# Decoder block on one core: order of loads at the turn to the last projection, a third pair of gate buffers, and the place of the last right operand's split

## The chip, the cores and the metric

The kernel runs on one core of a Trainium2 chip. The core has TensorE (PE) for matrix products, VectorE (DVE), ScalarE (ACT) and GpSimd (POOL) for elementwise work, SyncE (SP), which here only issues DMAs, and 16 DMA engines that all queues share. Each engine works through its own queue in order; semaphores tie the queues together. TensorE writes to eight banks of PSUM.

The metric is the device time of the program in microseconds (us), the median over runs. Before the change it is 2260.27 us, the median of 3 runs (2259.36 to 2262.28).

## The reference, cut to what matters

One layer, batch 1, 2048 positions, width 1024, all float32. What matters here is the end of it:

```python
proj = h @ w_in[l]
x_rnn, z_rnn, q, k, v, z_attn, g_r, g_a = jnp.split(proj, IN_SPLITS, axis=-1)
...
y_rnn = (hr * jax.nn.silu(z_rnn.astype(jnp.float32))).astype(dt) @ w_out_rnn[l]
...
o = dilated_attention_mixture(qh, kh, vh).reshape(B, S, D_ATTN)
y_attn = (o * jax.nn.silu(z_attn.astype(jnp.float32))).astype(dt) @ w_out_attn[l]
merged = jax.nn.sigmoid(g_r + bg_r) * y_rnn + jax.nn.sigmoid(g_a + bg_a) * y_attn
x = x + gate[:, None, :] * (merged @ w_o[l])
...
return rms_norm(x, g_final)
```

So there are three products of 2048 x 1024 by 1024 x 1024 at the end: the recurrent branch's output projection, the attention branch's, and the output product with `w_o`. Between them stand the two sigmoid gates and a sum.

## The kernel before

**Numbers.** A float32 product is made of three products on rounded halves: each operand is split into a high half (ScalarE, `hi_act`, line 158) and a low half, the rest (GpSimd `lo_pool`, line 164, or VectorE `lo_dve`, line 167). `mm3` then issues high·high, high·low and low·high (all through line 150). Tiles are 128 partitions by 512 float32, 256 KB.

**Stages.** First come norm, input projection and recurrence; their results go to DRAM scratch: the gated recurrent rows `yaT`, the sigmoid gates `grT` and `gaT`, and so on. Then attention, head by head; its gated outputs go to `oT`. Under attention and after it run the two output projections as fillers, and last the product with `w_o`, which uses seven products in place of eight for each 2 x 2 block (the names X, Z, W, V, Y are its PSUM banks).

**The fill, `steps` (lines 1781 to 1928).** It is a generator that issues one step of three matmuls at a time. Eight jobs, each 512 columns: jobs 0 to 3 project `yaT` and write `mrT` (recurrent branch times its gate), jobs 4 to 7 project `oT` and write `meT`, the merged sum. A job has eight tiles `m` of 128 output rows, and a tile has eight steps `k`, one for each block of 128 input rows. Jobs 0 to 5 go one after the other (tiles 0 to 47). The last two jobs, 6 and 7, share their weights and are interleaved (tiles 48 to 63): (6,0) (6,1) (7,0) (7,1) (6,2) (7,2) and so on to (6,6) (7,6) (7,7) (6,7). The change calls tile 47 `TURN`. PSUM banks alternate between two of a pool `pj`; among the last sixteen tiles every third and fourth uses the Z and W banks of the output products.

In each tile the generator also issues, at fixed steps and thus in a fixed place of each engine's queue:

- `load_w`: half a tile's weight, 512 KB, already split, from the scratch `wD`, two tiles ahead in halves (`u + 3`). It goes into one of four buffers S0 to S3 and must wait until the products that read the old content are done. From number 100 on (`RAW_W`) weights come unsplit (`rw`, three buffers) and are split on the spot (`split_w`).
- `load_y`, `split_y`: the 128 x 512 row blocks of the next job; some go through four raw buffers R0 to R3, each free when the split of its last content is done. Job 7's halves lie in the space of four right operands (`F`).
- `load_g(t)` at step 3: the gates of tile t, `grT` alone in jobs 0 to 3, later `gaT` and `mrT`, into four buffers `fg` (two pairs).
- `evict(t - 1)` (VectorE): PSUM times gate (line 1857), plus the recurrent part (line 1859), in place in the gate buffer.
- `store(t - 1)`: that buffer to `mrT` or `meT` (line 1864). Its buffer is free for a new load when the store has landed.

All these DMAs stand in the one queue of SP, in the order of issue. When one waits for its buffer, all behind it wait.

**The output products, `output_products` (lines 1943 to 2205).** While the last 128 steps (tiles 48 to 63) run, `steps_at` adds work at given steps: the seven right operands are loaded in 28 parts (`load_o`, four buffers `or`), in the order `B11, T2, T3, T1, B21, T4, B22`; parts of B11, B21 and B22 are multiplied by the residual gate (`gate_o`, VectorE, line 1976); then `hi_o` (ScalarE) and `lo_o` (even parts GpSimd, odd parts VectorE). The last operand, B22, is parts 24 to 27; its product is the last of each block, and for the first block it runs behind the first product of the second block. The left operands are read from `meT` (`raw`, line 2025), summed (lines 2036, 2037, 2046, 2048) and split, by the list `jobs`, which `run_jobs(n)` works off behind product n; negative numbers stand for steps of the fill. `load_x` brings the residual rows `xo` (line 2042). `add_x` (GpSimd, line 2169) and `finish` (VectorE, line 2108 or 2140) add the products to them; the sums u2 and u3 are lines 2182 and 2187.

The lines on which the change works, as they were:

```python
if k == 3:
    load_g(t)
...
if k in (1, 2):
    load_y(j + 1, k + 4)
if k == 2:
    load_y(j + 1, KT - 1)
...
late_parts = [(0, load_o, 27)]
for i in range(24, 28):
    late_parts += [(d + (i - 24) // 2, fn, i) for d, fn in ((1, gate_o), (2, hi_o), (3, lo_o))]
```

Of the kernel before, what the change touches and what calls it, by code (L numbers as in the profile page):

```python
# [20 lines left out]
P = 128  # L21
# [68 lines left out]
def decoder_block(ctx, tc, x, c, positions, g_norm, w_mod, b_mod, w_in, b_gate, conv_w, conv_b,  # L90
# [1690 lines left out]
    def steps(jobs):  # L1781
# [1 line left out]
        tiles = [(j, m) for j in range(LAST_HEAD) for m in range(KT)]  # L1783
        tiles += [(LAST_HEAD + i, m) for i in range(2) for m in range(2)]
        tiles += [(LAST_HEAD + (i ^ (m == KT - 1)), m) for m in range(2, KT) for i in range(2)]
        Y, G = {}, {}

        raw_at, split_at = {}, {}
        for x in range(RAW_W, 2 * KT * (LAST_HEAD + 1)):
# [55 lines left out]
        def load_g(t):  # L1845
            j, m = tiles[t]
            w, ys, n = jobs[j]
            at_ = slice(m * P, (m + 1) * P), slice(n * CH, (n + 1) * CH)
            G[t] = []
            for src in (grT,) if ys is yaT else (gaT, mrT):  # L1850
                g = T(fl, [P, CH], F32, "fg", bufs=4)
                nc.sync.dma_start(g[:], src[at_])
                G[t].append(g)

# [15 lines left out]
        for t, (j, m) in enumerate(tiles):  # L1870
            ps = T(pj, [P, CH], F32, "pj") if j < LAST_HEAD or t % 4 < 2 else FP["bank"](t % 4 - 2)
            for k in range(KT):
                u = 2 * t + k // KH
                if k % KH == 1:
                    if u + 3 < RAW_W - 1:
                        load_w(u + 3)
                    elif u == 2 * KT * LAST_HEAD:
                        load_w(RAW_W - 1)
                    if u in raw_at:
                        load_w(raw_at[u])  # L1880
                    if u in split_at:
                        split_w(split_at[u])
                if k == (1 if j < LAST_HEAD else 3) and t:
                    evict(t - 1, last)
                if k == 3:
                    load_g(t)
                if k == (7 if j < LAST_HEAD else 6) and t:
                    store(t - 1)
# [8 lines left out]
                if j < LAST_HEAD:  # L1897
                    if step in range(KT * KT - 24, KT * KT - 14, 2):
                        load_y(j + 1, (step - KT * KT + 24) // 2)
                    if step == KT * KT - KT - 1:  # L1900
                        split_y(j + 1, 0)
                    if m == KT - 1:
                        if k < 4:
                            split_y(j + 1, k + 1)
                        if j + 1 < LAST_HEAD:
                            if 4 <= k < KT - 1:
                                load_y(j + 1, k + 1)
                        else:
                            if k in (1, 2):
                                load_y(j + 1, k + 4)  # L1910
                            if k == 2:
                                load_y(j + 1, KT - 1)
                            if k == KT - 1:
                                split_y(j + 1, KT - 1)
                    if j and m == 0 and k in (0, 2, 3):
                        split_y(j, 5 + (k + 1) // 2)
                else:
                    i = (t - KT * LAST_HEAD) * KT + k
                    if i < 2:
                        split_y(j, 5 + i)  # L1920
# [22 lines left out]
    def output_products(fill):  # L1943
# [19 lines left out]

        def load_o(i):
            part, k = O_PART[B_ORDER[i // KH]], i % KH
            raw_o[i] = T(fp, [P, CH], F32, "or", bufs=4)
            if isinstance(part, int):
                nc.sync.dma_start(raw_o[i][:], oD[k, :, part, :])
            else:
                rows, cols = (slice(n * d, (n + 1) * d) for n, d in ((part[0] * KH + k, P), (part[1], CH)))  # L1970
                nc.sync.dma_start(raw_o[i][:], w_o[0, rows, cols])

        def gate_o(i):
            part = O_PART[B_ORDER[i // KH]]
            if not isinstance(part, int):
                tt(raw_o[i][:], raw_o[i][:], gate_b[:, part[1] * CH : (part[1] + 1) * CH], ALU.mult)

        def hi_o(i):
            name, k = B_ORDER[i // KH], i % KH
            if k == 0:  # L1980
                F[name] = f_tile(), f_tile()
            hi_act(F[name][0][:, k, :], raw_o[i][:])

        def lo_o(i):
            name, k = B_ORDER[i // KH], i % KH
            (lo_dve if i % 2 else lo_pool)(F[name][1][:, k, :], raw_o.pop(i)[:], F[name][0][:, k, :])
# [290 lines left out]
```

## Time and profile before

| | |
|---|---|
| median of 3 runs | 2260.27 us (2259.36 to 2262.28) |
| time of the profiled execution | 2258.11 us |
| its span, first to last instruction | 2256.0 us |
| granted clock of TensorE, mean | 0.992 |
| DMA, mean rate over the span | 231 GB/s |
| TensorE busy, 2000 to 2050 us of the span | 49.13 of 50 us |
| DMA engines busy, same stretch | 0.91, 280 GB/s |

Some names for reading the lines: `S<-wD` is a split weight, `rw<-in_w_out_attn_dram` a raw one, `R<-oT` a row block of attention outputs (in 1980 to 2010) and `R<-meT` a left operand, `fg<-gaT` and `fg<-mrT` the gate pair, `meT<-fg` the store of a finished tile, `or<-...` a part of a right operand, `F` a right operand's halves, `xo` the residual rows. "SPq" marks a DMA's issue on SP's queue, with start and length of the issue; the number in brackets at an instruction is the idle time of its engine just before it, with what ended it. Times count from the first instruction.

### The profile page before, as it was taken

What the parts mean: (1) busy time and instruction counts of PE and PEld (TensorE: products, weight loads), DVE (VectorE), ACT (ScalarE), POOL (GpSimd) and SP (SyncE); (2) the same over time, 40 slices, a digit from 0 to 9 for tenths busy, and PEclk for the clock granted to TensorE, in tenths of its full rate; (3) what the DMA queues carried; (4) which work ended last, traced back from release to release, by engine and by line L of the source; (5) the groups of instructions that cost most, each with busy time, mean ns of one, the idle gap of its engine ahead of it and who ended that gap; (6) DMA issues with size and microseconds to landing.
All of it is one profiled execution on the core that took longest, in us unless ns stands there. A gap on an engine that the chain in (4) does not pass through costs nothing.

```text
span 2256.0 us, 34354 instructions
## 1 busy us (share of the span) xinstructions
PE 2201.3 (98%) x11359; PEld 1845.6 (82%) x11359; DVE 1456.7 (65%) x2451; ACT 1294.0 (57%) x2560; POOL 1215.1 (54%) x902
## 2 busy tenths in 40 slices
PE   8999999999999999999999999999999999999898
PEld 5998888888877988888888887888989898977786
DVE  5578788778557664555645455467677878645776
ACT  3547767678533436666766611477677887632333
POOL 2277677676556344445445312356565656433786
PEclk9999999999999999999999999999999999999999
DMA  8354665565797647877787899989988888788553
GB/s 283 90 171 165 204 212 179 189 228 189 233 268 230 219 138 224 260 233 237 241 256 237 261 309 296 298 266 289 272 280 264 241 261 257 234 275 260 174 168 131
DMA packets 455433, 520.19 MB, mean 231 GB/s; under 512 B 90360, under 2 KB 333268, under 8 KB 454232
## 3 DMA queue, kind: packets, MB, share of 16 engines
q1 hardware_dynamic: 427492, 434.95, 63.6%
q10 hardware_dynamic: 27572, 83.00, 9.7%
q8 instruction: 90, 1.47, 0.3%
q14 instruction: 87, 0.71, 0.1%
q0 software_dynamic: 192, 0.05, 0.0%
HBM read 340.67 MB, written 177.21 MB: 230 GB/s over the span
## 4 chain that ended last, share of the span: by engine, by line
PE 48%; DMA 10%; DVE 3%; issue 3%; ACT 2%; POOL 2%; SPq 1%; ACTq 0%; POOLq 0%; DVEq 0%
PE X L150 9%; PE pj L150 9%; PE V L150 7%; PE W L150 4%; PE Z L150 4%; PE Y L150 4%; PE sc L150 4%; PE o L150 4%; DMA fg<-mrT 1%; DMA meT<-fg 1%; PE pg L150 1%; PE pT L1628 1%; DMA wo<-in_w_o_dram 1%; PE pT L1641 1%; DMA R<-in_w_in_dram 1%
## 5 line engine op out<-in xcount | busy, mean ns | idle before, releaser
L164 POOL TENSOR_TENSOR S<-R,S 128x512 fp32r<-128x512 f32 x278 | 408.2, 1473 | 402.8 <-ACT S L158 361.4
L150 PE MATMUL X<-T,S 128*128 128x512 f32 x1344 | 334.8, 398 | 10.4 <-ACT S L158 5.2
L150 PE MATMUL V<-T,S 128*128 128x512 f32 x1344 | 331.2, 395 | 0.0
L150 PEld LDWEIGHTS X<-T,S 128*128 128x128 f32 x1344 | 255.0, 190 | 72.1 <-ACT S L158 5.9
L150 PEld LDWEIGHTS V<-T,S 128*128 128x128 f32 x1344 | 252.3, 188 | 58.3 <-DVE ev L466 0.3
L150 PE MATMUL pj<-yh,S 128*128 128x512 f32 x848 | 287.8, 397 | 4.6 <-DMA S<-wD 3.9
L158 ACT ACTIVATE S<-R 128x512 fp32r<-128x512 f32 x278 | 170.7, 622 | 134.5 <-DMA R<-in_w_in_dram 111.8
L164 POOL TENSOR_TENSOR S<-s,S 128x512 fp32r<-128x512 f32 x108 | 165.9, 1537 | 128.7 <-ACT S L158 97.0
L150 PEld LDWEIGHTS pj<-yh,S 128*128 128x128 f32 x848 | 160.9, 190 | 37.9 <-DVE fg L1859 4.3
L1544 ACT ACTIVATE pp<-pp,st 128x256 f32<-128x256 f32 (+3 forms) x256 | 133.4, 523 | 75.2 <-DVE st L1543 74.8
L150 PE MATMUL pj<-yl,S 128*128 128x512 f32 x424 | 167.5, 395 | 2.1 <-DVE yl L167 1.2
L150 PE MATMUL Y<-T,S 128*128 128x512 f32 x672 | 165.5, 395 | 0.0
L150 PE MATMUL Z<-T,S 128*128 128x512 f32 x672 | 165.4, 395 | 0.0
L150 PE MATMUL W<-T,S 128*128 128x512 f32 x672 | 165.3, 395 | 0.0
L150 PEld LDWEIGHTS Z<-T,S 128*128 128x128 f32 x672 | 126.6, 188 | 29.7
L150 PEld LDWEIGHTS Y<-T,S 128*128 128x128 f32 x672 | 126.6, 188 | 29.3
L150 PEld LDWEIGHTS W<-T,S 128*128 128x128 f32 x672 | 126.4, 188 | 29.3
L158 ACT ACTIVATE S<-s 128x512 fp32r<-128x512 f32 x108 | 67.3, 623 | 109.7 <-DVE s L290 35.1
L167 DVE TENSOR_TENSOR ptl<-pT,pth 128x384 fp32r<-128x384 f32 (+1 forms) x160 | 97.8, 628 | 49.3 <-ACT pth L158 47.1
L960 DVE SCALAR_TENSOR_TENSOR xc<-xr,par,xc 128x512 f32<-128x512 f32 x96 | 96.6, 1006 | 50.2 <-ACT xc L954 48.0
L1543 DVE CUSTOM_DVE_ANT_0 pp<-sc,msk 128x256 f32<-128x256 f32 (+3 forms) x256 | 104.2, 449 | 37.2 <-PE sc L150 35.0
L164 POOL TENSOR_TENSOR kq<-kraw,kq 128x512 fp32r<-128x512 f32 (+1 forms) x64 | 101.3, 1593 | 41.7 <-ACT kq L158 41.7
(382 smaller groups left out, 4841.6 us busy)
## 6 DMA issues: line engine op xcount, KB each, us to landing
sD<-S ACTq DMA_DIRECT2D x118, 512.0 KB, 3.7
S<-sD SPq DMA_DIRECT2D x118, 512.0 KB, 5.1
S<-wD SPq DMA_DIRECT2D x100, 512.0 KB, 5.7
R<-in_w_in_dram SPq DMA_DIRECT2D x196, 256.0 KB, 4.1
wD<-s ACTq DMA_DIRECT2D x64, 256.0 KB, 4.9
T<-in_w_mod_dram SPq DMA_DIRECT2D x8, 1024.0 KB, 12.0
vN<-ev SPq DMA_DIRECT2D x64, 128.0 KB, 2.8
zaT<-ev SPq DMA_DIRECT2D x32, 256.0 KB, 2.8
```

What stands on the lines that cost most here:

```text
L150: nc.tensor.matmul(o, lhsT=l, rhs=r, start=st, stop=sp, **kw)
L158: nc.scalar.activation(o, i, AF.Copy)
L164: nc.gpsimd.tensor_tensor(o, i, h.bitcast(F32), ALU.subtract)
L167: nc.vector.tensor_tensor(o, i, h.bitcast(F32), ALU.subtract)
L960: nc.vector.scalar_tensor_tensor(xc, xr[:, i : i + CH], cw(i), xc, ALU.mult, ALU.add)
L1543: nc.vector.tensor_tensor_reduce(pdst, s_ps, mask, 1.0, 3e38, ALU.add, ALU.min, m_)
L1544: nc.scalar.activation(pdst, pdst, AF.Exp, bias=m_, scale=-1.0, accum_out=l_)
L1628: nc.tensor.transpose(pt[:, c0 + j * P : c0 + (j + 1) * P], pp[i][:, k * P : (k + 1) * P], ident)
L1641: nc.tensor.transpose(pt[:, c * P : (c + 1) * P], pp[:, half * P : (half + 1) * P], ident)
```

## The change

Three edits, all in the order and place of work that exists already. No product, elementwise operation or byte of DMA is added or taken away.

1. At tile 47 the weight number 98 (first half of tile 49) is loaded at step 3 behind that step's products, ahead of row block 6 of job 6; it was loaded at step 5, behind row blocks 5 and 6 and tile 47's gates. Row block 6 moves from step 2 to step 3 (block 7 of that job needs no load, its rows are still in SBUF). Tile 47's gates move from step 3 to step 4.
2. Tiles 50, 53, 56, 59 and 62 take a third pair of gate buffers, one free slot each of the split rows `yh` and `yl`; the other tiles go on with the two pairs. From tile 50 on, a tile's gates are loaded at the end of the tile before (behind its step 7) and not at its own step 3.
3. Parts 24 to 26 of the right operands are loaded at steps 105, 107 and 109 of the last 128, into the three buffers of the raw weights, gated at 113, 115 and 117, and split at 124 to 127; they were loaded at steps 124 to 126 and gated and split behind the first four output products. Part 27 is loaded at step 123 and not after the last step; its gating and split stay behind products 2 to 4. The splits of parts 20 to 23 go one step earlier.

```diff
-        Y, G = {}, {}
+        Y, G, spare_g = {}, {}, []
+        TURN = KT * LAST_HEAD - 1
...
             G[t] = []
-            for src in (grT,) if ys is yaT else (gaT, mrT):
-                g = T(fl, [P, CH], F32, "fg", bufs=4)
+            if t == TURN + 3:
+                spare_g.extend(T(fl, [P, CH], F32, tag, bufs=NY) for tag in ("yh", "yl"))
+            for i, src in enumerate((grT,) if ys is yaT else (gaT, mrT)):
+                g = spare_g[i] if t > TURN and (t - TURN) % 3 == 0 else T(fl, [P, CH], F32, "fg", bufs=4)
                 nc.sync.dma_start(g[:], src[at_])
...
                     if u + 3 < RAW_W - 1:
-                        load_w(u + 3)
+                        if u + 3 == n_w[0]:
+                            load_w(u + 3)
...
-                if k == 3:
+                if k == (4 if t == TURN else 3) and t < TURN + 3:
                     load_g(t)
...
-                            if k in (1, 2):
-                                load_y(j + 1, k + 4)
-                            if k == 2:
+                            if k == 1:
+                                load_y(j + 1, 5)
+                            if k == 3:
+                                load_w(n_w[0])
+                                load_y(j + 1, 6)
                                 load_y(j + 1, KT - 1)
...
+                    if k == KT - 1 and TURN + 2 <= t < len(tiles) - 1:
+                        load_g(t + 1)
                 yield
...
-            raw_o[i] = T(fp, [P, CH], F32, "or", bufs=4)
+            if i in range(24, 27):
+                raw_o[i] = T(fp, [P, KH, P], F32, "rw", bufs=3)[:].rearrange("p k m -> p (k m)")
+            else:
+                raw_o[i] = T(fp, [P, CH], F32, "or", bufs=4)[:]
...
             if i >= 20:
-                at_step(101 + i, lambda i=i: hi_o(i))
-                at_step(102 + i, lambda i=i: lo_o(i))
-                if i > 20:
-                    at_step(103 + i, lambda i=i: load_o(i + 3))
+                at_step(100 + i, lambda i=i: hi_o(i))
+                at_step(101 + i, lambda i=i: lo_o(i))
...
+        for i in range(24, 27):
+            at_step(57 + 2 * i, lambda i=i: load_o(i))
+            at_step(65 + 2 * i, lambda i=i: gate_o(i))
+            at_step(100 + i, lambda i=i: hi_o(i))
+            at_step(101 + i, lambda i=i: lo_o(i))
+        at_step(123, lambda: load_o(27))
...
-        late_parts = [(0, load_o, 27)]
-        for i in range(24, 28):
-            late_parts += [(d + (i - 24) // 2, fn, i) for d, fn in ((1, gate_o), (2, hi_o), (3, lo_o))]
-        for d, fn, n in late_parts:
-            jobs.append((d, len(jobs), lambda fn=fn, n=n: fn(n)))
+        for d, fn in ((2, gate_o), (3, hi_o), (4, lo_o)):
+            jobs.append((d, len(jobs), lambda fn=fn: fn(27)))
```

More of the change, by code (lines that the diff above doesn't have):

```diff
@@ L1965, in load_o @@
             part, k = O_PART[B_ORDER[i // KH]], i % KH
-            raw_o[i] = T(fp, [P, CH], F32, "or", bufs=4)
+            if i in range(24, 27):
+                raw_o[i] = T(fp, [P, KH, P], F32, "rw", bufs=3)[:].rearrange("p k m -> p (k m)")
+            else:
+                raw_o[i] = T(fp, [P, CH], F32, "or", bufs=4)[:]
             if isinstance(part, int):
-                nc.sync.dma_start(raw_o[i][:], oD[k, :, part, :])
+                nc.sync.dma_start(raw_o[i], oD[k, :, part, :])
             else:
                 rows, cols = (slice(n * d, (n + 1) * d) for n, d in ((part[0] * KH + k, P), (part[1], CH)))
-                nc.sync.dma_start(raw_o[i][:], w_o[0, rows, cols])
+                nc.sync.dma_start(raw_o[i], w_o[0, rows, cols])
         def gate_o(i):
@@ L1975, in gate_o @@
             if not isinstance(part, int):
-                tt(raw_o[i][:], raw_o[i][:], gate_b[:, part[1] * CH : (part[1] + 1) * CH], ALU.mult)
+                tt(raw_o[i], raw_o[i], gate_b[:, part[1] * CH : (part[1] + 1) * CH], ALU.mult)
         def hi_o(i):
@@ L1981, in hi_o @@
                 F[name] = f_tile(), f_tile()
-            hi_act(F[name][0][:, k, :], raw_o[i][:])
+            hi_act(F[name][0][:, k, :], raw_o[i])
         def lo_o(i):
             name, k = B_ORDER[i // KH], i % KH
-            (lo_dve if i % 2 else lo_pool)(F[name][1][:, k, :], raw_o.pop(i)[:], F[name][0][:, k, :])
+            (lo_dve if i % 2 else lo_pool)(F[name][1][:, k, :], raw_o.pop(i), F[name][0][:, k, :])
         B_ORDER = "B11", "T2", "T3", "T1", "B21", "T4", "B22"
```

## The prediction

> **What bounds the kernel now.** I read the page first: the span, and a TensorE that is busy 98% of it. So there is only its idle time to win, and I asked for the waits of TensorE from the end of attention on (total us, times, longest). Then I cut that part of the span into stages (length, busy time and count of each engine, granted clock, DMA share, GB/s).
>
> ```profile
> span 2256.0 us, 34354 instructions
> PE X L150 <- POOL S L164: 4.2, 1, 4.2
> PE pj L150 <- DMA S<-wD: 3.9, 1, 3.9
> PE Z L150 <- DVE fg L1857: 1.5, 1, 1.5
> PE W L150 <- DVE fg L1857: 1.2, 1, 1.2
> 1985.00:1990.00 5.00, 5.00 (x24) 4.14 (x23) 2.19 (x3) 1.26 (x2) 1.72 (x2) 1.00 0.89 217
> 1995.00:2000.00 5.00, 4.86 (x14) 3.87 (x15) 0.69 (x1) 1.89 (x3) 1.60 (x2) 0.66 0.99 382
> 2058.00:2081.60 23.60, 23.60 (x104) 19.23 (x103) 12.65 (x17) 4.20 (x7) 5.12 (x4) 1.00 0.86 247
> 2081.60:2115.00 33.40, 26.04 (x97) 19.48 (x96) 22.60 (x25) 14.48 (x29) 23.58 (x16) 0.90 0.70 219
> 2115.00:2245.30 130.30, 130.30 (x567) 106.34 (x566) 94.10 (x162) 49.72 (x118) 104.55 (x70) 1.00 0.48 150
> ```
>
> Two places stand out: one weight wait of 3.9 us at the turn to the last projection, with the clock at 0.66 behind it, and the start of the output products, 2081.6 to 2115, with the other waits and a clock of 0.90. Behind 2115 TensorE never waits; a matmul takes 130.30/567 = 0.230 us there, a product of 12 of them 2.76 us. The timeline of the turn, with two pieces of the chain of waits and the landing time of one load at its end:
>
> ```profile
> 1982.44 1.65 SPq L359 DMA_DIRECT2D R<-oT  x2
> 1984.14 0.90 SPq L1750 DMA_DIRECT2D oT<-zt  x2
> 1986.57 0.49 SPq L353 DMA_DIRECT2D S<-wD  x1
> 1988.01 1.29 POOL L164 TENSOR_TENSOR yl<-R,yh 128x512 fp32r<-128x512 f32 x1 [2.58 <-ACT yh L158]
> 1995.14 0.47 PE L150 MATMUL pj<-yh,S 128*128 128x512 f32 x1 [3.93 <-DMA S<-wD]
> 2002.30 4.83 PE L150 MATMUL Z<-F,S 128*128 128x512 f32 x19
> 2007.81 0.63 ACT L158 ACTIVATE F<-R 128x512 fp32r<-128x512 f32 x1 [2.13 <-DMA R<-oT]
> 2009.78 5.74 PE L150 MATMUL W<-F,S 128*128 128x512 f32 x24
> 2011.96 1.74 POOL L164 TENSOR_TENSOR S<-rw,S 128x512 fp32r<-128x512 f32 x1
> 2015.35 0.39 PE L150 MATMUL pj<-yh,S 128*128 128x512 f32 x1
> 2070.58 5.76 PE L150 MATMUL Z<-F,S 128*128 128x512 f32 x24
> 2076.18 0.39 PE L150 MATMUL W<-yh,S 128*128 128x512 f32 x1
> ...
> 1987.16 8.52 DMA meT<-fg
> 1995.74 6.45 DMA R<-oT
> R<-oT SPq DMA_DIRECT2D x1, 256.0 KB, 3.2
> ```
>
> A tile normally lasts 2076.18 − 2070.58 = 5.60 us (5.45 with yh operands: 2076.18 to 2081.63 below). Tile 49 starts 3.93 us late, at 1995.14, and with the slow clock takes 2002.30 − 1995.14 = 7.16 us, 1.71 too many. Tile 50 takes 2009.78 − 2002.30 = 7.48, 1.88 too many, since its rows of attention output arrive in drops, the last at 2007.81. Lost at the turn: 7.52 us. The start of the products:
>
> ```profile
> 2019.05 4.47 DMA meT<-fg
> 2023.58 4.58 DMA fg<-mrT
> ...
> 2078.52 0.47 SPq L1852 DMA_DIRECT2D fg<-gaT  x1
> 2081.63 2.96 PE L150 MATMUL X<-F,S 128*128 128x512 f32 x12
> 2095.14 0.42 SPq L1971 DMA_DIRECT2D or<-in_w_o_dram  x1
> 2101.39 0.63 PE L150 MATMUL X<-F,S 128*128 128x512 f32 x2
> 2101.44 0.69 DVE L1976 TENSOR_TENSOR or<-or,gate_b 128x512 f32<-128x512 f32 x1 [4.49 <-DMA or<-in_w_o_dram]
> 2102.82 1.64 POOL L2169 TENSOR_TENSOR xo<-xo,u 128x512 f32<-128x512 f32 x1 [7.01 <-DVE u L2182]
> 2104.42 1.71 POOL L164 TENSOR_TENSOR S<-R,S 128x512 fp32r<-128x512 f32 x1
> 2106.18 4.63 PE L150 MATMUL X<-F,S 128*128 128x512 f32 x10 [4.16 <-POOL S L164]
> 2115.02 2.94 PE L150 MATMUL Z<-F,S 128*128 128x512 f32 x12
> ```
>
> From 2081.63 to 2115.02 stand eight products; 33.39 us for 8 × 2.76 = 22.06. Lost there: 11.33 us. How: part 27 of the right operands is loaded only at 2095.14; its gating (L1976) stands at the head of VectorE's queue and holds it for 4.49 us; behind it is the sum u2, on that waits GpSimd's addition (7.01 us idle), behind that stands the low half of the next left operand (L164), and on that waits TensorE. The part is late because the SP queue is: tile 62's gates were due three steps into tile 62, 2070.58 + 3 × 0.70 = 2072.7, and went out at 2078.52, 5.8 us late. The queue is late because mrT's load waits for the buffer that an earlier tile's store is leaving: store 4.47, load 4.58, an addition and two issues make some 10.3 us for two tiles of 11, so a backlog from the turn is never worked off.
>
> **The change, part by part.** *Weight 98 ahead.* It moves from step 5 to step 3 of tile 47, ahead of row block 6 of the attention outputs and of tile 47's gates (these go from step 3 to 4). Its buffer is free when step 3 of tile 47 is done: tile 48 ended at 1995.14 − 3.93 = 1991.21, so tile 47 at 1985.76, four steps of 0.68 before that is 1983.0. Row 5 goes out at 1982.44, the two stores that follow no longer wait for block 6's buffer and take 0.90, so the weight leaves at 1983.8 instead of 1986.57, and block 6 at 1984.3 instead of about 1983.9, but with 1 MB (two stores, one weight) newly ahead of it. Tile 48 needs block 6 two steps before its end, at 1989.85. Landing is not shown for this order: lower bound 3.2 us as for its neighbour, so 1987.5, plus 0.63 and 1.29 for the two halves 1989.4, no wait; upper bound 8.5 us as the store of 1987.16, so 1994.7, a wait of 4.9. I take 3.2 + 1 MB at 382 GB/s = 5.8, as the queue is less crowded than at 1987: 1992.0, a wait of 2.2 in place of 3.93.
>
> That does not decide the turn. Tile 50 needs its last row block, loaded through the buffer of block 3 of the same set, which went out (1995.74) only when the store of 1987.16 had landed and freed a gate buffer. This pair has no third buffer yet. Everything on SP comes some 1.2 us sooner (stores at 1982.9, not 1984.14), so the last block is there at 2006.6 and tile 50 ends at 2008.6: gain 1.2. Bounds: if block 6 meets its upper bound and the clock drops again, tile 50 starts 1 us later, −1; from above, tile 52's raw weight is ready at 2011.96 + 1.74 = 2013.7 for a start at 2015.35, 1.65 us to spare, so at most 1.2 + 1.65 = 2.9 while the queue runs as now.
>
> *Third pair of gate buffers.* No instruction is added. Tiles 50, 53, 56, 59, 62 use a free slot pair of the split rows; from tile 50 on gates are asked for at the end of the tile before, four steps (2.8 us) sooner, ahead of that tile's raw weight, part and store on SP. The cycle of 10.3 us now has 16.5 us; SP runs on time within some six tiles. The waits for tiles 62's and 63's gates (1.5 and 1.2 us, part of the 11.33) go.
>
> The Trainium skill, DMA: Bandwidth & Descriptors, section Anatomy of one DMA — SWDGE (gpsimd) path, puts a DMA at about 2.0 us plus bytes over 436 GB/s, for these 256 KB an estimate of 2.6; by that, store and load would make 5.2 us, the queue would be on time with two pairs, the third would bring nothing, and the sum would lack the 2.7 us of the two gate waits. The trace disagrees with 4.47 and 4.58, and decides.
>
> *The last right operand.* Parts 24 to 26 go from the products to steps 105 to 127, in buffers of the raw weights (their last split is at step 97); part 27 is loaded at step 123. Nothing is added: three gatings, three high and three low halves move ahead of the first product, and parts 20 to 23 go one step earlier. Their prices (ns min/median/max, and landing):
>
> ```profile
> L158 ACT ACTIVATE F<-or x28: 613/632/634, 2010.0 to 2102.2; 128x512 fp32r<-128x512 f32 x28
> L164 POOL TENSOR_TENSOR F<-or,F x14: 1279/1293/1743, 2010.7 to 2112.4; 128x512 fp32r<-128x512 f32 x14
> L1976 DVE TENSOR_TENSOR or<-or,gate_b x12: 679/692/1776, 2009.3 to 2101.4; 128x512 f32<-128x512 f32 x12
> DMA to landing us min/median/max: 3.9/5.1/6.7
> ```
>
> ScalarE, VectorE and GpSimd are busy 4.20, 12.65 and 5.12 of the 23.60 us before the products, so 1.9, 2.8 and 2.6 us more are covered by tiles 60 to 63. What is late next? GpSimd, in order from tile 63's start (5.45 us before the first product): low half of left operand 1, parts 20, 22, left operand 2, parts 24, 26, left operand 3. At 1.75 us each, from 0.7 us in, the seventh is done 7.5 us after the first product starts; the fourth product needs it at 8.3. Carried on so, with the addition of 1.64, the next block's first operand is done at 16.2 and needed at 16.6. If that cover is gone, TensorE stops there at once. Loads: gates and stores of four tiles, eight parts and six left operands, 26 of 0.25 MB, are 6.5 MB in these last 22 us, 295 GB/s against 247 served now and 382 at the turn. Bounds for what is left of the 11.33: nothing (as behind 2115), or 3.5 us (6.5 MB at 247 GB/s are 26.3 us, less 22, less than one product's slack). I take 0.5, nearer to the stage that never waits: gain 10.8.
>
> **Sum.** 1.2 + 10.8 = 12.0 us. The profiled execution took 2258.11 (its span 2256.0 and 2.11 around it); less 12.0 it is 2246.1. The median of the runs is 2.16 above it, so 2248.3 is forecast for the median.
>
> **Rivals.** *Half of it stays (0.16).* The fuller start of the products makes a new wait, on GpSimd or on a load, and the clock drops: as before 4.16 us idle made ten matmuls take 4.63 instead of 2.30. With a wait of 3.3 and 2.3 for the clock, 5.6 go back: 2254. For it speaks the 0.4 us to spare; against it that GpSimd is idle for most of tiles 60 to 63. The Trainium skill, TensorE: Matmul & The Clock Gate, section What's actually happening, has the clock halve only after an idle window of about 3.4 us; by that a wait of 3.3 can pass at full clock and this rival costs 3.3, an estimate of 2251.6. The trace agrees as far as 1.5 and 1.2 us cost no clock and 3.93 did.
>
> *The turn clears too (0.10).* The 217 GB/s of 1985 to 1990 were an accident, the stores land early, and 6 of the 7.52 us go: 2243.5.
>
> *It doesn't do what it says (0.06).* The backlog of the turn lasts, a spare pair every third tile only moves the wait to the other pairs; VectorE still waits for a late part: 2260.3 − 1.2 = 2259.
>
> *Slower (0.08).* SP stays as late as now, 5.8 us, and the early parts with it. Then three gatings stand in VectorE's queue ahead of the first left operand's sums, three high halves ahead of ScalarE's and two low halves ahead of GpSimd's: 2.1 + 0.7 + 1.9 + 3.5 = 8.2 us in front of the fourth product, none covered, while the old loss stays: 2260.3 − 1.2 + 8.2 = 2267. It decides once parts 24 to 26 land after tile 62's end. Against it: these loads are issued at steps 105 to 109 and gated at 113 to 117, eight steps or 5.6 us for a median landing of 5.1.
>
> **How the numbers follow.** The forecast has 0.60, its own range 2244.5 to 2252. The range 2243.5 to 2257 leaves out the slower case, the one without effect, and a part of the best: 0.18. A measurement of this kernel tells 0.2%, 4.5 us, from no change. Faster: 0.60 + 0.10 and three quarters of 0.16, 0.82; same: the rest of that and most of the case without effect, 0.09; slower 0.09.
>
> **What will show it.** Right: no wait of TensorE between the first X product and the second Z, these eight products in about 22.5 us at clock 1.00; no idle time of VectorE before L1976 for part 27; tile 62's gates issued before tile 62 starts; a short wait in tile 48 where tile 49 waited, and tile 50 still slow. Wrong: a weight or row wait at the turn longer than before, or a GpSimd low half that holds the fourth or seventh product.

## The result, and the profile after

| | before | after |
|---|---|---|
| median of 5 runs each | 2260.27 us (2259.27 to 2262.32) | 2251.73 us (2248.68 to 2253.62) |
| profiled execution, and its span | 2258.11, 2256.0 | 2252.32, 2250.5 |
| ratio after to before | | 0.9956, 95% interval 0.9944 to 0.9967 |

By the medians the change makes the kernel 8.5 us (0.38%) faster. The ratio of 0.9956 means 9.9 us, and its interval 7.5 to 12.7. Forecast were 12.0 us and 2248.3; by the medians the size is 3.4 us short.

The two profiled executions differ by 5.8 us only. In the one of after, attention ended 3.01 us later than in the one of before (1981.06 against 1978.05); over all executions profiled in this study that instant lies anywhere from 1974 to 1987 us, with kernels whose attention is the same. So I compare pieces behind it, each measured inside one execution:

| piece | before | after | difference |
|---|---|---|---|
| turn: end of attention to the first matmul of tile 51 | 31.73 | 30.37 | −1.36 |
| tiles 51 to 63 | 71.85 | 71.89 | +0.04 |
| start: first X product to second Z product, 22.06 without a wait | 33.39 | 26.22 | −7.17 |
| from there to the end | 140.95 | 140.94 | −0.01 |

The sum is 8.50. That it meets the difference of the medians (8.54) so closely is chance, since the five times of each kernel lie 3 to 5 us apart. The waits of TensorE from 1960 on, in the changed kernel (total us, times, longest):

```profile
PE W L150 <- DVE fg L1860: 2.1, 1, 2.1
PE pj L150 <- ACT yh L158: 1.6, 1, 1.6
PE pj L150 <- POOL yl L164: 0.8, 1, 0.8
```

Of the four waits of before, none is left in its old form; the weight wait of 3.9 is gone, both gate waits of 1.5 and 1.2 and the 4.2 for the low half. New are a short wait in tile 48 for row block 6, and one of 2.1 for VectorE's eviction of tile 63 (`fg`, line 1860). The stages:

```profile
1995.00:2000.00 5.00, 4.22 (x12) 3.33 (x13) 1.38 (x2) 0.92 (x2) 2.00 (x2) 0.66 1.03 404
2059.70:2083.30 23.60, 23.60 (x104) 19.23 (x103) 15.14 (x20) 5.17 (x9) 6.46 (x4) 1.00 0.96 266
2083.30:2110.00 26.70, 24.64 (x99) 19.44 (x98) 22.53 (x22) 13.51 (x28) 26.34 (x17) 0.94 0.72 218
2088.79:2092.20 3.41, 1.34 (x7) 0.81 (x6) 3.37 (x5) 1.24 (x3) 3.41 (x3) 1.00 0.54 182
2092.20:2095.61 3.41, 3.41 (x10) 2.66 (x9) 3.41 (x4) 1.15 (x2) 3.41 (x3) 0.50 0.65 192
```

Ahead of the products the DMA engines are now busy at 0.96 (0.86 before). From 2083.3 to 2110 GpSimd has hardly a gap (26.34 of 26.70). VectorE is busy for 22.53 of it, and from 2088.79 to 2095.61 almost throughout (3.37 and 3.41 of 3.41). Behind each of the two idle times of TensorE the clock is low: 0.66 in the mean from 1995 to 2000, and 0.50 from 2092.20 to 2095.61. The turn, in the timeline of after:

```profile
1986.81 0.44 SPq L353 DMA_DIRECT2D S<-wD  x1
1987.34 0.48 SPq L359 DMA_DIRECT2D R<-oT  x1
...
1994.43 0.50 PE L150 MATMUL pj<-yh,S 128*128 128x512 f32 x1 [1.57 <-ACT yh L158]
1995.78 0.50 PE L150 MATMUL pj<-yl,S 128*128 128x512 f32 x1 [0.85 <-POOL yl L164]
2004.10 4.70 PE L150 MATMUL Z<-F,S 128*128 128x512 f32 x19
2011.43 5.73 PE L150 MATMUL W<-F,S 128*128 128x512 f32 x24
...
2009.45 0.63 ACT L158 ACTIVATE F<-R 128x512 fp32r<-128x512 f32 x1 [2.29 <-DMA R<-oT]
```

Weight 98 leaves ahead of row block 6. TensorE now waits for that block, and tile 50 still takes 2011.43 − 2004.10 = 7.33 us, since its last row block is split only at 2009.45. The start of the products, in the same timeline:

```profile
2069.71 0.33 SPq L1982 DMA_DIRECT2D rw<-in_w_o_dram  x1
2072.26 5.76 PE L150 MATMUL Z<-F,S 128*128 128x512 f32 x24
2076.62 0.32 SPq L1855 DMA_DIRECT2D yh<-gaT  x1
2077.33 0.69 DVE L1987 TENSOR_TENSOR rw<-rw,gate_b 128x512 f32<-128x512 f32 x1 [6.00 <-DMA rw<-in_w_o_dram]
2078.90 0.69 DVE L1987 TENSOR_TENSOR rw<-rw,gate_b 128x512 f32<-128x512 f32 x1 [0.88 <-DMA rw<-in_w_o_dram]
2081.44 0.69 DVE L2052 TENSOR_TENSOR s<-R,R 128x512 f32<-128x512 f32 x1
2083.32 2.96 PE L150 MATMUL X<-F,S 128*128 128x512 f32 x12
2084.13 1.36 DVE L167 TENSOR_TENSOR F<-or,F 128x512 fp32r<-128x512 f32 x1 [0.68 <-ACT F L158]
2087.13 1.78 DVE L167 TENSOR_TENSOR F<-or,F 128x512 fp32r<-128x512 f32 x1
2088.83 1.76 DVE L167 TENSOR_TENSOR F<-rw,F 128x512 fp32r<-128x512 f32 x1
2090.51 0.68 DVE L1860 TENSOR_TENSOR fg<-W,fg 128x512 f32<-128x512 f32 x1
2091.34 4.58 PE L150 MATMUL W<-F,S 128*128 128x512 f32 x12 [2.06 <-DVE fg L1860]
2109.53 2.72 PE L150 MATMUL Z<-F,S 128*128 128x512 f32 x11
```

The third product writes to bank W, in which tile 63 lies until VectorE has evicted it. VectorE is late: at 2077.33 the first gating of B22 has held it for 6.00 us, since part 24, issued at 2069.71, lands some 7.6 us later; from the second gating on it works with no pause but one of 0.68, and the last low half ahead of the eviction is that of part 25 (`F<-rw`). TensorE idles for 2.06 us, and the row of that product shows 4.58 us where one at full clock shows 2.96 (the first, at 2083.32): 1.62 more. That is 3.7 of the 26.22 − 22.06 = 4.16 us that are left.

The third pair does its part. The waits of SP's own queue from 2000 to 2085, before and then after (L1852 and L1855 are the same line, the load of a gate):

```profile
SPq L1852 <- DMA meT<-fg: 23.2, 8, 3.9
```

```profile
SPq L1855 <- DMA meT<-yh: 2.1, 2, 1.8
SPq L1855 <- DMA meT<-fg: 1.0, 1, 1.0
```

The 23.2 us that gate loads waited for a store to land have become 3.1. SP waits elsewhere now: 13.9 us (9.8 and 4.1) before stores, for VectorE's sum of the tile (line 1862). There it waits for data and not for a buffer: the queue has caught up with the tiles in these places.

### The profile page after: what moved, and what is told of

The parts are those of the page before. It is cut to its first block, busy times and chain, and to the rows that moved or that the text cites. A ratio compares the mean times of both kernels' runs of the same rounds, so it can differ in the third digit from the quotient of the medians.

```text
span 2250.5 us, 34360 instructions
## 1 busy us (share of the span) xinstructions
PE 2200.9 (98%) x11358; PEld 1847.0 (82%) x11359; DVE 1463.0 (65%) x2451; ACT 1294.7 (58%) x2560; POOL 1220.9 (54%) x902
## 4 chain that ended last, share of the span: by engine, by line
PE 51%; DMA 8%; DVE 4%; ACT 2%; issue 2%; SPq 1%; POOL 1%; ACTq 0%; DVEq 0%; POOLq 0%
PE pj L150 10%; PE X L150 9%; PE V L150 8%; PE W L150 5%; PE Z L150 5%; PE o L150 4%; PE sc L150 4%; PE Y L150 4%; PE pT L1628 1%; PE pg L150 1%; DMA wo<-in_w_o_dram 1%; DMA fg<-mrT 1%; PE pT L1641 1%; DMA or<-oD 1%; DMA mrT<-fg 1%
## 5 line engine op out<-in xcount | busy, mean ns | idle before, releaser
L150 PEld LDWEIGHTS W<-T,S 128*128 128x128 f32 x672 | 126.4, 188 | 29.3
```

The lines of the kernel that those rows point to most:

```text
L150: nc.tensor.matmul(o, lhsT=l, rhs=r, start=st, stop=sp, **kw)
```

## The experiments

My first theory: edit 1 wins the 1.4 us of the turn; edit 2 alone wins most of the start; what is left comes from the early gating that holds VectorE for 6 us. The rivals: the place of parts 24 to 27 (edit 3) does it; what is left is the amount of B22's early work on the engines, or the loads, with the DMA engines full.

**Each edit alone.** Each kernel is the one before with one edit of the diff shown above.

```diff
e1: +                            if k == 3:
    +                                load_w(n_w[0])
    +                                load_y(j + 1, 6)
e2: +                g = spare_g[i] if t > TURN and (t - TURN) % 3 == 0 else T(fl, [P, CH], F32, "fg", bufs=4)
    +                    if k == KT - 1 and TURN + 2 <= t < len(tiles) - 1:
    +                        load_g(t + 1)
e3: +            at_step(57 + 2 * i, lambda i=i: load_o(i))
    +            at_step(65 + 2 * i, lambda i=i: gate_o(i))
```

> The first edit alone: weight 98 ahead of row block 6, nothing else. Turn = from the end of attention's last sum on TensorE to the start of tile 51 (before 31.73 us, changed kernel 30.37); start = from the first output product to the second Z product (33.39 and 26.21). Theory: the 1.36 us won at the turn belong to this edit, so turn 30.4 and start as before, 33.4; about 1.4 us faster in all, 0.9994. Rival: the turn differs by chance of the two executions, turn 31.7.

> The second edit alone: third pair of gate buffers and gates asked for at the end of the tile before. Theory: the backlog of the SP queue made part 27 and the last gates late, so this edit alone wins most of the start: turn 31.7, start 24 to 28 us, 5 to 9 us faster, 0.9965 to 0.998. Rival: the place of parts 24 to 27 is what counts; then the start stays at 30 us or more and the kernel is at most 3 us faster.

> The third edit alone: parts 24 to 26 loaded, gated and split under the last tiles, part 27 loaded at step 123. Theory: without the third gate pair the SP queue is some 6 us late, the early parts land later still, and their three gatings hold VectorE ahead of the last gates and of the left operands' sums: turn 31.7, start 28 to 33 us, at most 5 us faster. Rival: only the place of part 27 counted; then start 26 us and about 7 us faster, 0.997.

| kernel | median | ratio to before, interval | turn | start |
|---|---|---|---|---|
| edit 1 alone | 2258.3 | 0.9988 (0.9976 to 1.0) | 29.40 | 35.28 |
| edit 2 alone | 2248.43 | 0.9943 (0.9926 to 0.996) | 31.10 | 26.02 |
| edit 3 alone | 2255.09 | 0.9975 (0.9962 to 0.9988) | 31.20 | 28.64 |

The gate pair alone brings the start from 33.39 to 26.02, as far as all three edits (26.22), and with them its kernel is as fast as the changed one within the intervals. Edit 3 alone wins 4.8 there, but nothing on top of edit 2. Edit 1 alone shortens the turn and no more; its start, 35.28 in the one execution profiled, is as full of waits as before. For edit 2 the two pieces make 0.63 + 7.37 = 8.0 us, and its ratio 12.9 (9.0 to 16.7): some of that gain does not show in these pieces of one execution, and no run says where it is. Waits of TensorE with edit 2 alone, from 1960 on:

```profile
PE pj L150 <- DMA S<-wD: 3.1, 1, 3.1
PE V L150 <- DVE xo L2145: 1.9, 1, 1.9
PE V L150 <- POOL F L164: 1.1, 1, 1.1
```

Its timeline at tile 62, with the issue of that tile's gates:

```profile
2069.81 5.76 PE L150 MATMUL Z<-F,S 128*128 128x512 f32 x24
2071.11 0.64 SPq L1855 DMA_DIRECT2D yh<-gaT  x1
```

The weight wait of the turn stays without edit 1 (3.1). The gates of tile 62 leave 1.3 us behind its start; before the change it was 7.9 (2078.52 − 2070.58), in the changed kernel it is 4.4 (2076.62 − 2072.26). At the start it is B22's late split, behind the products, that TensorE waits for (V, 1.9 and 1.1). With all three edits that wait is gone, and the one for the eviction stands in its place.

**The gating later.** Parts 24 to 26 are gated at steps 119, 121 and 123, six steps later than in the change, so that VectorE does not stand before them.

```diff
-            at_step(65 + 2 * i, lambda i=i: gate_o(i))
+            at_step(71 + 2 * i, lambda i=i: gate_o(i))
```

> The changed kernel with the gatings of parts 24 to 26 at steps 119, 121 and 123 in place of 113, 115 and 117, behind the sums of the first left operand. Theory: what is left of the loss at the start (26.21 against 22.06) comes from the first of these gatings, which held VectorE for 6.00 us for its load; behind it the work ran into the products. Moved back it waits little: start 22.1 to 24 us, no wait of the W product for tile 63's eviction, 2 to 4 us faster than the changed kernel, 0.994 to 0.9955 of before. Rival: the early splits are too much work for VectorE and GpSimd in that stretch wherever the gatings stand; then start 25.5 us or more, no gain.

2250.9 us, 0.9949 (0.9931 to 0.9968), start 27.33: no gain. VectorE in this kernel, and its first product:

```profile
2075.94 0.69 DVE L2052 TENSOR_TENSOR s<-R,R 128x512 f32<-128x512 f32 x1 [1.85 <-DMA R<-meT]
2077.27 0.68 DVE L1987 TENSOR_TENSOR rw<-rw,gate_b 128x512 f32<-128x512 f32 x1
2078.47 1.79 DVE L1987 TENSOR_TENSOR rw<-rw,gate_b 128x512 f32<-128x512 f32 x1
2080.75 2.96 PE L150 MATMUL X<-F,S 128*128 128x512 f32 x12
2081.89 1.78 DVE L1987 TENSOR_TENSOR rw<-rw,gate_b 128x512 f32<-128x512 f32 x1
2089.05 0.68 DVE L1860 TENSOR_TENSOR fg<-W,fg 128x512 f32<-128x512 f32 x1
```

The sums of the first left operand start 4.8 us before the first product, and not 1.9 as in the changed kernel. But all three gatings, 0.68 + 1.79 + 1.78 = 4.25 us, now stand between them and the eviction, which comes 8.3 us behind the first product's start (7.2 in the changed kernel). That the wait at the gating is the whole cause, my first theory, is thereby refuted: the wait goes, the work takes its place, and the start is no shorter.

**No B22 at all.** Parts 24 to 27 are neither loaded nor gated nor split; the product reads the halves of B21.

```diff
-            (bh, bl), t = F[name], first.pop(i)
+            (bh, bl), t = F["B21" if name == "B22" else name], first.pop(i)
```

> The changed kernel without the last right operand's work: parts 24 to 27 are not loaded, gated or split, and the last product of each block reads B21's halves in place of B22's (so a quarter of the output product's last term is another one). Theory: the 4 us that are left at the start (26.2 against 22.06) are B22's own work, which lands on VectorE and GpSimd around the first products: start 22 to 23.5 us. Rival: they come from loads, the left operands' rows above all, which land late because the DMA engines are full before the products; then the start stays at 25 us or more.

2244.05 us, 0.9927 (0.9906 to 0.9948), start 22.23: nothing is left to win there. So the 4 us are B22's own.

**Its loads, or its work.** Two kernels take B22 apart: one loads parts 24 to 27 as in the change and does nothing with them; the other gates and splits as in the change, but on the buffers of parts 20 to 23, without the four loads.

```diff
loads:  -            at_step(65 + 2 * i, lambda i=i: gate_o(i))
        -            at_step(100 + i, lambda i=i: hi_o(i))
        -            at_step(101 + i, lambda i=i: lo_o(i))
work:   +            if i >= 24:
        +                raw_o[i] = T4[i - 4]
        +                return
```

> The changed kernel with parts 24 to 27 of the right operands loaded as in the change, but neither gated nor split; the product with B22 reads the halves of B21 in their place, so this leaves out four gatings and eight halves and no DMA. The question: of the 4 us that the first eight products still lose in the changed kernel (26.2 us from the first X product to the second Z product, 22.1 without a wait; 22.2 when B22's parts are neither loaded nor worked on), how much comes from the four loads and how much from the work on the engines? Theory A, the loads: these 1 MB stand in a stretch where the DMA engines are full (0.92 to 1.05 busy), all landings grow late, so it stays at 25 us or more. Theory B, the engines: VectorE and GpSimd have no time left beside tile 62's and 63's evictions, so without the work it is 22 to 23.5 us and the time that of the run without B22, some 2244 to 2246 us.

> The converse: the changed kernel with the gatings and halves of parts 24 to 27 at their places in the change, but on the buffers that hold parts 20 to 23, so that four loads of 256 KB are left out (the result is computed from other numbers). Theory A, the loads: without them the work finds its data early and VectorE is not held at its first gating: 22 to 23.5 us for the first eight products, some 2245 us. Theory B, the engines: the same work in the same queues, so 25 us or more, as in the changed kernel, some 2250 us.

The loads alone: 2245.08 us, 0.994 (0.9923 to 0.9957), start 22.23. The work alone: 2245.58 us, 0.9939 (0.9921 to 0.9958), start 23.08. Neither costs much by itself (0.2 and 1.0 us above 22.06); together they cost 4.16, of which 1.6 are the clock's. The full DMA engines are no cause as such: with all loads in place (0.98 busy, 289 GB/s from 2057 to 2081) the first three products follow each other without a gap:

```profile
2080.17 2.96 PE L150 MATMUL X<-F,S 128*128 128x512 f32 x12
2082.96 2.96 PE L150 MATMUL Z<-F,S 128*128 128x512 f32 x12
2085.76 2.96 PE L150 MATMUL W<-F,S 128*128 128x512 f32 x12
```

VectorE with the work alone, and its first product:

```profile
2074.65 0.69 DVE L1990 TENSOR_TENSOR or<-or,gate_b 128x512 f32<-128x512 f32 x1 [4.47 <-DMA or<-oD]
2077.19 0.68 DVE L2055 TENSOR_TENSOR s<-R,R 128x512 f32<-128x512 f32 x1
2081.36 2.95 PE L150 MATMUL X<-F,S 128*128 128x512 f32 x12
2086.28 0.68 DVE L1860 TENSOR_TENSOR fg<-W,fg 128x512 f32<-128x512 f32 x1
```

The eviction comes 4.92 us behind the first product's start, where the change has 7.19: 2.27 apart. From the sums to the eviction both take the same, 9.09 and 9.07. All of the difference lies ahead of the sums: VectorE stood 4.47 us before a gating here and 6.00 + 0.88 = 6.88 in the change, 2.41 more. The third product can start 5.6 us behind the first (2085.76 − 2080.17 with the loads alone), and it follows the eviction's start by 0.83 (2091.34 − 2090.51), so the eviction is due by 4.8. The work alone meets that within 0.15 us; waiting for its data 2.4 us longer, it misses by 2.4. Here then is what the forecast lacked: VectorE has just room for B22's early work, if the parts are there in time; when they are 2.4 us later, its whole queue is, down to the eviction of tile 63.

**Shorter landings?** The left operands are read in rows of 512 bytes. This kernel reads 128 whole rows of 2 KB for each instead, the same bytes (other numbers are read).

```diff
-                nc.sync.dma_start(v[name], meT[half * KH * P : (half + 1) * KH * P, c0 : c0 + P]
-                                  .rearrange("(k p) m -> p k m", p=P))
+                r0 = (half * KH + r + i) * P
+                nc.sync.dma_start(v[name].rearrange("p k m -> p (k m)"), meT[r0 : r0 + P, n * CH : (n + 1) * CH])
```

> The changed kernel with each left operand's load reading 128 whole rows of 2 KB of the merged sum in place of 512 rows of 512 bytes: the same 256 KB, other numbers are read (so the output is of other operands). If the DMA engines are full before the products because of the short pieces (250 to 290 GB/s moved there, against 370 GB/s in 2050 to 2060), landings in 2055 to 2081 fall back from 7 to about 5 us and the first eight products take 22.1 to 24.5 us in place of 26.2. If the loads are not what is late, it stays at 25.5 or more; the rest of the products, where DMA is half idle, stays at 140.9 us either way.

2248.51 us, 0.9953 (0.9936 to 0.997), start 25.16. The DMA queue and one load, from 2055 to 2081, first in the changed kernel, then in this one:

```profile
DMA packets 6390, 7.44 MB, mean 286 GB/s; under 512 B 455, under 2 KB 3527, under 8 KB 6390
rw<-in_w_o_dram SPq DMA_DIRECT2D x3, 256.0 KB, 7.5
```

```profile
DMA packets 4602, 7.49 MB, mean 288 GB/s; under 512 B 455, under 2 KB 1116, under 8 KB 4601
rw<-in_w_o_dram SPq DMA_DIRECT2D x3, 256.0 KB, 7.2
```

With 28% fewer packets the rate is the same, parts 24 to 26 land after 7.2 us and not 7.5, and the left operands' own loads after 8.6 and not 8.0. The third product waits for the eviction as long as in the changed kernel:

```profile
2089.87 3.04 PE L150 MATMUL W<-F,S 128*128 128x512 f32 x12 [2.07 <-DVE fg L1860]
```

What is shorter is the product itself, 3.04 against 4.58, since the clock did not drop here behind an idle time as long (more on this under "The clock"); that is where the 1.1 us of the start come from, less some 0.5 lost in the products behind it. The length of the pieces does not explain the late landings. What does limit the rate there stays open.

**The turn in another order.** The spare pair goes to tiles 48, 51, 54 and so on, and row block 6 back to step 2, ahead of the weight; the first kernel has the rest of the change, the second has B22's parts loaded as before the change and split two products later still.

```diff
-            if t == TURN + 3:
+            if t == TURN + 1:
...
-                g = spare_g[i] if t > TURN and (t - TURN) % 3 == 0 else T(fl, [P, CH], F32, "fg", bufs=4)
+                g = spare_g[i] if t > TURN and (t - TURN) % 3 == 1 else T(fl, [P, CH], F32, "fg", bufs=4)
...
-                                load_y(j + 1, 6)
```

> The changed kernel with the third gate pair two tiles earlier (tiles 48, 51, 54 and so on) and row block 6 loaded at step 2 again, ahead of the weight. Theory: what bounds the turn is the SP queue: tile 48's gates wait for a store, and behind them wait job 7's row blocks; with a free pair these go out some 6 us sooner and block 6 no longer arrives late, so the turn falls from 30.4 to 26.5 to 28.5 us; start as in the changed kernel, 26 to 27.5. Rival: the DMA engines are full at the turn whatever the order; turn 30 to 31.

> The orders of the last two runs together: third pair from tile 48 on, row block 6 ahead of the weight, parts 24 to 27 worked on two products later. Theory: both gains add, turn 26.5 to 28.5 and start 22.5 to 24.5 us, 12 to 16 us faster than before, 0.993 to 0.995. Rival: one eats the other, since more is asked of the DMA engines at once; then not faster than the third gate pair alone, 0.9943.

The turn takes 30.05 and 29.76 us, no better than with edit 1 as it is: 29.3 to 30.9 in the nine kernels that have it. Both theories fail. The start takes 26.41 us, and 28.40 in the second kernel, where 22.5 to 24.5 had been expected. The times are 2248.3, 0.9952 (0.9935 to 0.9969), and 2251.12, 0.9963 (0.995 to 0.9975). TensorE no longer waits for block 6 there, and waits 1.9 us instead, in both kernels, for the eviction of tile 47, for whose gates VectorE stands 4.95 and 4.31 us. Whichever load goes first, another is late: from 1995 to 2000 the DMA engines are full in both (1.04 busy, 394 and 400 GB/s), as in the changed kernel (1.03, 404).

**The parts later, or as before.** Edits 1 and 2 with B22's parts loaded as before; in the first kernel they are gated and split two products later than before the change, in the second as before it.

```diff
before: +            late_parts += [(d + (i - 24) // 2, fn, i) for d, fn in ((1, gate_o), (2, hi_o), (3, lo_o))]
later:  +            late_parts += [(d + (i - 24) // 2, fn, i) for d, fn in ((3, gate_o), (4, hi_o), (5, lo_o))]
```

> The first two edits, with parts 24 to 27 loaded as before the change but gated, split high and split low two products later than there (behind products 3, 4, 5 and one more for parts 26 and 27), behind the sums u2 and the next block's first operand. Theory: with the third gate pair alone the start was 26.0 because the gatings still hold VectorE ahead of u2; behind it they cost nothing: start 22.5 to 24.5 us, turn 30. Rival: VectorE and GpSimd are full there in any order; start 26 us.

> Edits 1 and 2 of the change without edit 3: weight 98 ahead, third gate pair, parts 24 to 27 loaded, gated and split as before the change. If the effects of the edits add up as the single runs say, the turn takes 29.4 to 30.4 us as with edit 1 (31.1 with edit 2 alone) and the first eight products 26.0 as with edit 2 alone: some 2247 to 2249 us, ratio 0.9935 to 0.995, no slower than the changed kernel, and edit 3 is worth nothing beside edit 2. If edit 3 is needed once the gates are early, the first eight products take over 27.5 us and the time is 2251.5 or more.

Later: 2251.62 us, 0.9969 (0.9957 to 0.9982), start 27.05. As before: 2249.35 us, 0.9956 (0.9939 to 0.9973), turn 30.52, start 24.61. Waits of TensorE when the parts come later:

```profile
PE V L150 <- POOL F L164: 3.0, 2, 2.5
```

Now GpSimd's low halves of B22 are what the V products wait for, so this theory fails too. Wherever B22's twelve operations stand in the kernels with the third pair and all loads, 2.5 to 6.3 us are lost in the start (24.61 to 28.40 against 22.06). The kernel without edit 3 is as fast as the changed kernel, so edit 3 brings nothing that could be measured beside edit 2. In the profiled executions their starts differ by 1.61 us (24.61 and 26.22), as much as the lower clock costs in the changed kernel. No kernel that computes the reference was shown to beat the changed one: edit 2 alone has 0.9943, and the intervals overlap.

One order was not tried: the early gatings as in the change, with the low half of part 25 (1.76 us) behind the eviction of tile 63. By the account above, and as an estimate only, it would take 1.8 of the 2.4 us that VectorE is late.

## Why the prediction was right, and where it was wrong

**What bounds the kernel, and the two places.** Right: tiles 51 to 63 and the rest kept their lengths within 0.04 us, and all of the gain that the pieces show lies in the turn and the start.

**Weight 98 ahead: 1.2 forecast, 1.36 measured.** Weight and row block were to leave at 1983.8 and 1984.3; with attention's end 3.01 later they left at 1986.81 and 1987.34, which is 1983.80 and 1984.33. The wait for block 6 was put at 2.2 and is 1.57 + 0.85 = 2.42. That the turn is decided by tile 50's last row block, and not by this wait, held too: that block was forecast there for 2006.6, and its split starts at 2009.45 − 3.01 = 2006.44. The gain is not chance of one execution: nine kernels with edit 1 have a mean of 29.96 us (29.27 to 30.89), three without it 31.34 (31.10 to 31.73).

**Third gate pair.** The mechanism held: TensorE's gate waits are gone, SP's waits for stores fell from 23.2 to 3.1 us, and edit 2 alone shows both (there 4.6). "SP runs on time within some six tiles" failed for the last gates. That tile 62's gates are issued before tile 62 starts was wrong in the changed kernel: they leave at 2076.62, 4.4 us behind its start (7.9 before). With edit 2 alone it is 1.3; three early loads of parts stand ahead of them in the changed kernel. The Trainium skill's fit that the prediction draws on is, by the title of its section, one for DMAs on GpSimd's path; the DMAs here stand in SP's queue, and store and load took 4.47 and 4.58 us, and the rival by which the third pair brings nothing failed: edit 2 alone shortens the start by 7.37.

**The last right operand: the step that failed.** "I take 0.5, nearer to the stage that never waits: gain 10.8." Measured are 4.16 us left and a gain of 7.17, outside the two bounds (nothing and 3.5). That 2251.73 still lies within the forecast's own range (2244.5 to 2252), by 0.3 us, is luck as far as this term goes, which was 3.6 us too high. Two parts of its working failed:

- "so 1.9, 2.8 and 2.6 us more are covered by tiles 60 to 63": for VectorE, the 2.8, this was read from its busy time, 12.65 of 23.60. The idle time was not free: VectorE stood in it before loads. I followed the order of GpSimd's queue operation by operation, and not VectorE's, in which tile 63's eviction stands behind the sums and the low halves and is due 4.8 us after the first product starts. With the data 2.4 us sooner (the work alone) the work fits, with 1.0 us lost. The 2.8 are also four operations at 0.69 us; the low half of part 25 took 1.76, beside a busy GpSimd.
- Landing. "a median landing of 5.1" was taken for parts 24 to 26 against eight steps or 5.6 us; they landed after 7.5. The rate was bounded (247 to 382 GB/s, it became 266 to 286), but its lateness was spent on TensorE's data only, and not on an engine's queue that waits in order.

The credit was also put on the wrong edit. I saw that part 27 is late because SP is, and still gave the gain to moving the split. The gates alone bring 7.37 us; between B22's late split (3.96 left with edit 2 alone, 2.55 with edits 1 and 2) and its early one (4.16) no run shows a gain for the early one.

**The rivals.** "Half of it stays" came halfway: a new wait at the fuller start with the clock drop behind it, 3.7 us against the 5.6 it was given, on VectorE and not on GpSimd or a load for TensorE. "The turn clears too" failed: the turn still takes 30.37 us, and the DMA engines are full there. "It doesn't do what it says" failed by SP's 3.1 us. The slower case's condition, parts landing after tile 62's end (2072.26 + 5.60 = 2077.86), was met by part 25, for which VectorE waited until 2078.90. It did not cost what was put on it, because the old loss did not stay.

**The clock.** I cited the Trainium skill, TensorE: Matmul & The Clock Gate, section What's actually happening, for a wait of 3.3 us that may pass at full clock. The runs do not bear out that a wait must be so long: behind 2.06 us of idle time the changed kernel's product took 4.58 us, behind 2.07 that of the kernel with whole rows took 3.04. What differs is where the wait lies. In the clock rows of all fourteen traces, from 1900 to 2235 us, a stretch at half clock lasts 3.41 or 6.83 us, and within one execution these stretches start on a grid of 3.41 us, whose place differs between executions. In the changed kernel the whole wait lies in one step of the grid, 2088.79 to 2092.20, in which TensorE is busy for only 1.34 of 3.41 us, and the next step has a clock of 0.50 (both lines are shown above). With whole rows the grid, counted on from the half clock at the turn, cuts the wait: 1.87 us of idle time in the one step, 0.20 in the next, and no drop.

```profile
2086.26:2089.67 3.41, 1.54 (x7) 0.92 (x5) 3.41 (x3) 1.53 (x4) 3.41 (x3) 1.00 0.66 235
2089.67:2093.08 3.41, 3.21 (x14) 2.56 (x14) 3.38 (x4) 0.54 (x1) 3.41 (x3) 1.00 0.38 115
```

From 1900 to 2235 us the same holds in all fourteen traces: behind each of the 18 full-clock steps in which TensorE was idle for 1.89 us or more, the clock dropped, and behind none of the others. Earlier in the kernel, among matmuls of other shapes, the two groups overlap between 0.94 and 1.91 us. The same section calls the window, in which the activity is watched, free-running; the grid agrees with that, but a drop behind a step that was idle for 1.89 of 3.41 us does not agree with an idle window of about 3.4. So 1.6 of the 4.16 us left are a price that other executions of the same order need not pay, since it is chance where the grid lies.

## What to carry to other kernels

An engine's idle time in a stage is cover only if the work can be done in it: write out the queue of each engine that gets new work, in order, up to the first operation for which another engine waits, with its due time, and add the time by which that work's own data are late. Of several edits on one chain, ask what each is worth when the others are already there; here the buffer pair that let the DMA queue run ahead was worth the whole gain at the start, and the moved split nothing beside it. A load moved into a full stretch lands by the full stretch's times (7.5 us here), not by the median of such loads over a longer one (5.1 from 1995 to 2115 before the change).

## What the runs showed of the hardware that was not expected

VectorE's operation on two operands in SBUF takes 0.69 us alone and 1.76 to 1.79 while GpSimd works (the gatings of 2077.27 and 2078.47 above, one kernel and one shape). An eviction, with one operand in PSUM, stays at 0.68 beside a busy GpSimd (2090.51). GpSimd pays as well, 1.29 alone (at 2072.13 in the changed kernel, with VectorE idle) and some 1.7 beside VectorE:

```profile
2088.32 1.72 POOL L164 TENSOR_TENSOR S<-R,S 128x512 fp32r<-128x512 f32 x1
2090.00 3.40 POOL L164 TENSOR_TENSOR F<-rw,F 128x512 fp32r<-128x512 f32 x2
```

From 2087.13 to 2088.83 VectorE starts one such operation in 1.70 us, and GpSimd one in 1.68 (2088.32 to 2090.00): a pair takes less than 0.69 + 1.29 = 1.98. The Trainium skill, SBUF — State Buffer, section SBUF: two separate sides, lets the two share a pair of ports, which a VectorE operation with two SBUF inputs or a GpSimd operation holds for its whole length while the other is blocked. The trace agrees on which operations meet (the eviction is spared); the 1.70 us for a pair are somewhat less than a strict turn-taking would need. For the sums: a low half or gating moved beside a busy GpSimd costs 1.8 us of VectorE and not 0.7, which is the other reason why the later gatings won nothing.
